# A decoder layer on TensorE: down weights' sums moved into the channel stage, gate weights' parts into the down stage, the first norm into the sixth product, and another order of the pre-products

## The chip, the cores and the metric

The kernel runs on one core of a Trainium2 chip. The metric is the device time of one execution in microseconds (us). PE stands for TensorE (PEld its weight loads), DVE for VectorE, ACT for ScalarE, POOL for GpSimd, SP for SyncE, which here only issues DMAs.

## The reference

One layer of a hybrid decoder (D_MODEL 1024, D_FF 2816) over 1024 prompt tokens and 8 x 4 sample tokens, 1056 together. After the mixing sub-layer (attention and a pooling mixer) come the parts that the change touches:

```python
f = _rms(x, n_ffn_pre)
f = (jax.nn.silu(f @ w_gate) * (f @ w_up)) @ w_down
x = x + _rms(f, n_ffn_post)
x = x + jax.nn.sigmoid(x @ w_ple_gate) * (p @ w_ple)
```

## The kernel before, in words

**Products.** Every fp32 product is made of three passes: each operand is split into a high part, a cast to the matmul type on ACT (`hi`, L185), and a low part, the difference on DVE (`lo`, L186); `gemm` (the matmuls stand at L135) issues hi*hi, hi*lo and lo*hi. Tile names tell the use: wh, wl split weights; sh, sl split sums of weights; qh, ql down weights; w the second weight half of a chunk; xo an activation operand of the down stage; eh one of the gate stage; hl the split of a norm's sum.

**Seven products for eight.** The channel, down and gate stages multiply 2 x 2 blocks by Strassen's scheme in Winograd's form: seven block products P1 to P7, of which four have sums of weight quarters S1 to S4 (`quarter_sums`) and four have sums of activation quarters T1 to T4 as operands. Tokens are cut in two halves of 528 (two matmuls of 264 columns), features in two halves.

**Channel stage.** 22 chunks of 256 channels of D_FF (22 x gate and up). Products P1 and P2 need no sums; they are made ahead, in 44 *pre-products* (`ahead`, L1161): each has a first half (12 matmuls, copied to `st`, L1167) and a second half (`rest`, another 12, copied at L1174 and stored to DRAM, `pd`). Second halves wait in a list; before, a call first issues its own first half and then takes old second halves until 2 (from the eighth call on 1) are left. Split weights live in a pool of 4 pairs, raw ones (wr) in 3 buffers; a split waits for PE to be done with the pair that it overwrites. Then `chunk` (L1204) loads p for chunk c + 2, applies Silu to chunk c's gate part (L1209) and makes the five other products (`seven`). The raw weights' sums are made on POOL (L1124), four operations of 128x512 a chunk, after DVE has made the split `w` from the same buffer; both sums are then split (sh, sl). Results go to DRAM as operands of the down stage (`chunk_put`, L1094). After chunks 3, 7, 11 and 15 `gate_sums` makes on POOL the four sums of a pair of gate weight blocks (tiles ws) and stores them to DRAM (`gd`).

**Down stage.** Seven products of 264 matmuls each, in the order P1, P2, S2, S3, P4, S1, S4 (named by their weights), over 11 slabs taken in groups (`down`, L1301). `x_get` loads the operand of a slab six slabs ahead and splits it. The weight forms of S2, S3, S1 and S4 are made in place on POOL (`down_form`, L316), out of quarters loaded again and one kept for each group. P1 and P2 accumulate in the same four bank pairs, which ACT copies out (L1357, L1359); S2 and all later products take fresh pairs, so they need those copies. The result of the first half of the tokens is complete after P4; its sum of squares is folded and the norm's mean is made by a matmul inside S1 (`rstd_steps`, hl at L421, L422). After S1, `alpha_steps` makes the norm and the gate stage's operands. The second half of the tokens follows after S4 (`beta_steps`).

**Gate stage.** For each of four pairs, P1 and P2 with directly loaded and split weights (W1), then forms S4, S1, S2, S3 and P4 (W2), loaded from `gd` and split in the stage. Sigmoid, product with the embedding, and the store follow.

The order on each engine is set by a scheduler from program order and waits, except for instructions marked `keep_in_program_order`; `turn`, `step` and `chain` spread norm and operand steps over matmuls by rough costs.

Of the kernel before, what the change touches and what calls it, by code (L numbers as in the profile page):

```python
# [17 lines left out]
P = 128  # L18
# [51 lines left out]
def trunk_kernel(  # L70
# [128 lines left out]
    in_a = set()  # L199

    def w_load(j):
        if j >= len(plan) or j in raws:
            return
        src, shape = plan[j]
        t = act_tile(shape) if j in in_a else wpool.tile(shape, F32, tag="wr", bufs=W_RAW, name=nm("wr"))
        queue(nc.sync.dma_start(t, src))
        raws[j] = t
# [57 lines left out]
    QUARTERS = {"P1": ("11", "22"), "P2": ("12", "21"), "S2": ("11",), "S3": ("11", "21"), "P4": ("22",), "S1": ("11",), "S4": ("12",)}  # L265
    OPERAND = {"P1": "B11", "P2": "B21", "P4": "T4", "S2": "T2", "S3": "T3", "S1": "T1", "S4": "B22"}
    WDN, DN_LOADS = {}, {}
    for k in DOWN:
        for e, ps in enumerate(SETS):
            js = []  # L270
            for q in QUARTERS[k]:
                r, c = int(q[1]) - 1, int(q[0]) - 1
                src = w_dn[ps[0] : ps[0] + len(ps), c, :, r, :].rearrange("s p n -> p s n")
                js.append(add_plan(src, [P, len(ps), 512]))
            if k == "P1":
                in_a.add(js[1])
            DN_LOADS[k, e] = tuple(js)
            WDN[k, e] = item("down", k, e)

    PAIRS = ((5, 4), (7, 6), (1, 0), (3, 2))  # L280
    FORMS = ("S2", "S4", "S3", "S1")

    def embed_item(h):
        return direct_item(w_ple[h], [P, 2, 512])

    gate_d = [dpool.tile([P, 4, 2, 512], F32, name=nm("gd")) for _ in range(2)]

    def form_item(k, g):
        if k == "P4":
            b = PAIRS[2 * g][1]  # L290
            src = w_pg[b : b + 3 : 2, :, 4:8, :].rearrange("s p k n -> p s k n")
        else:
            src = gate_d[g][:, FORMS.index(k)].rearrange("p s (k n) -> p s k n", n=P)
        return direct_item(src, [P, 2, 4, P])

    WE, W1 = {}, {}
    for a, _ in PAIRS:
        if a in (5, 1):
            WE[a // 4] = embed_item(a // 4)
        W1[a] = direct_item(w_pg[a], [P, KC, P])  # L300
    LATE = ("S4", "S1", "S2", "S3", "P4")
    W2 = {k: [form_item(k, g) for g in range(2)] for k in LATE}

    made = {}
    until = [len(ITEMS)]
    keeps = {}

    def plans(kind, js):
        return DN_LOADS[js] if kind == "down" else js

    def down_form(k, e):

        r = [raws[j] for j in DN_LOADS[k, e]]

        def add(out, a, b, op):
            ge.tensor_tensor(out, a, b, op=op)  # L316

        if k == "P1":
            keeps[e] = r[1]
        elif k == "P2":  # L320
            add(keeps[e], keeps[e], r[1], ALU.add)
        elif k == "S2":
            add(keeps[e], keeps[e], r[0], ALU.subtract)
            r = [keeps[e]]
        elif k == "S3":
            add(r[0], r[0], r[1], ALU.subtract)
        elif k == "S1":
            add(r[0], keeps[e], r[0], ALU.add)
        elif k == "S4":
            add(r[0], r[0], keeps[e], ALU.subtract)  # L330
        hl = w_tile(r[0].shape, "qh"), w_tile(r[0].shape, "ql")
        split(*hl, r[0])
        return hl

    def need(k, ahead=LOOK):

        for i in range(len(made), max(k + 1, min(k + ahead + 1, until[0]))):
            kind, js = ITEMS[i]
            for j in plans(kind, js):
                w_load(j)  # L340
# [3 lines left out]
            elif kind == "half":  # L344
                t = w_tile([P, KC, P], "w2")
                made[i] = t[:, 0:4, :], t[:, 4:8, :]
                split(*made[i], raws[js[0]][:, 4:8, :])
            elif kind == "down":
                made[i] = down_form(*js)
            else:  # L350
                made[i] = w_sums(*(raws[j] for j in js))
            for kind, js in ITEMS[i + 1 : i + 3]:
                for j in plans(kind, js):
                    w_load(j)
# [635 lines left out]
    def ffn_steps(g):  # L990

        r = yield from rstd_steps(acc[g])
# [168 lines left out]
    def ahead(w, c, i):  # L1161

        wg = need(w)
# [40 lines left out]
    def chunk(c):  # L1204
# [4 lines left out]
        se.activation(c11, c11, AF.Silu)  # L1209
# [62 lines left out]

    def gate_sums(n):

        a, b = PAIRS[n]
        two = []
# [4 lines left out]
        quarter_sums(*two)  # L1281
        for i, t in enumerate(two):
            nc.sync.dma_start(gate_d[n // 2][:, 2 * i : 2 * i + 2, n % 2, :], t.rearrange("p (f k) n -> p f (k n)", f=2))
# [17 lines left out]
    def down(k, banks, onto=False, ends=None, order_=(0, 1, 2, 3), behind=None, far=6):  # L1301

        n0 = DOWN.index(k) * NSLAB
        for es in ((0,), (1,), (2,), (3,), (4, 5)):
# [7 lines left out]
            for j in order_:  # L1312
# [12 lines left out]
                if 5 in es:  # L1325
                    ends(j, banks[j])
                    if behind:
                        behind(j)
# [15 lines left out]
    psum[0] = ctx.enter_context(tc.tile_pool(name="pairs", bufs=4, space=bass.MemoryType.PSUM))  # L1344
    for c in range(FFC):
# [4 lines left out]
        if c % 4 == 3 and c // 4 < len(PAIRS):  # L1350
            gate_sums(c // 4)

    share[0] = 0.5
    queued[:] = [None]
    u = out_half()
    banks = [None] * 4
    down("P1", banks, ends=lambda j, ps: se.copy(at_j(u, j), ps))  # L1357
    os_[0][0] = c11 = out_half()
    down("P2", banks, onto=True, ends=lambda j, ps: se.copy(at_j(c11, j), ps))  # L1359
    sq = half_squares(c11)  # L1360
    down("S2", [None] * 4, ends=lambda j, ps: add(at_j(u, j), at_j(u, j), ps))
    u3 = out_half()
    down("S3", [None] * 4, ends=lambda j, ps: add(at_j(u3, j), at_j(u, j), ps))
    os_[0][1] = c21 = out_half()
    down("P4", [None] * 4, ends=lambda j, ps: add(at_j(c21, j), at_j(u3, j), ps))

    sq2 = half_squares(c21)
    add(sq, sq, sq2)
    folded(0, sq)
    norm = rstd_steps(acc3[0])  # L1370
    next(norm)
    ordered[0] = True
    p5 = out_half()

    def p5_end(j, ps):
        se.copy(at_j(p5, j), ps)

    def norm_behind(j):
        if j == 2:
            next(norm)  # L1380

    down("S1", [None] * 4, ends=p5_end, behind=norm_behind)
    try:
        next(norm)
    except StopIteration as e:
        r = e.value
    ordered[0] = False
    for o in (u3, u):
        for t in range(2):
            add(o[t], o[t], p5[t])  # L1390
    os_[1] = [u, u3]

    def alpha_steps():
        for h in range(2):
            x2_load(0, h)
        for h in range(2):
            operand_tiles(f"B{h + 1}1")
            for t in range(2):
                x2_make(0, h, t, r)
                yield 18, 0  # L1400
                operand_split(f"B{h + 1}1", t, x2[0][h][t])
                yield 8, 0
        ple_operand(0)
        yield 8, 0
        sqb = half_squares(u3)
        folded(1, sqb)
        yield 16, 0

    chain(alpha_steps(), 0)

    def u_end(j, ps):
# [4 lines left out]
        sq = row("sq")  # L1416
        se.activation(sq, v, AF.Square)
        add(by_row(acc3[1]), by_row(acc3[1]), sq)

    down("S4", [None] * 4, ends=u_end, order_=(1, 2, 3, 0), far=4)  # L1420
# [40 lines left out]
    def beta_steps():  # L1461

        norm = rstd_steps(acc3[1])
        next(norm)
        yield
# [54 lines left out]
    for a, _ in PAIRS:  # L1520
        w = need(W1[a], 2)
        ps = product(quarter(w, 0), e7["B11"])
# [12 lines left out]
    for k in LATE:  # L1535
        for g in range(2):
            for i in range(2):
                a, b = PAIRS[2 * g + i]
                w = tuple(t[:, i] for t in need(W2[k][g], 1))
# [124 lines left out]
```

## Time and profile before

| | |
|---|---|
| runs | 1083.18, 1085.08, 1088.99 us |
| median | 1085.08 us |
| profiled execution | 1087.13 us |
| its span, mean granted clock of PE | 1085.3 us, 0.988 |
| PE, DVE, ACT, POOL busy | 97%, 72%, 44%, 25% |
| stages, us from the span's start | attention to 264; pre-products 264 to 407; chunks 409 to 732; down stage to 963; gate stage to the end |
| DMA | 201.75 MB, mean 186 GB/s |

A row of a window gives its length, then busy time and instructions of the engines asked for, the granted clock as a share of full speed, the DMA share and the rate. A row of a timeline gives start, duration, engine, line, operation, output and inputs, and in brackets the idle time ahead of it with what ended it. A row of waits gives total, count and longest. A group's row gives busy time and mean ns, then the idle time before. A DMA row ends with the median us from issue to landing.

### The profile page before, as it was taken

To read this page: it belongs to the slowest core of one execution; us is meant where nothing else is said; L and a number is where in the kernel's file an instruction comes from. 1 tells how busy PE (TensorE), PEld (TensorE's weight loads), DVE (VectorE), ACT (ScalarE), POOL (GpSimd) and SP (SyncE) were. 2 spreads that over 40 slices of the span, in tenths; PEclk is the share of its full clock that TensorE was granted. 3 is DMA by queue.
4 is the path that set the end of the run, shared out by engine and by line. 5 is a ranking of instruction groups with operands and counts; after the bars stand their busy time and mean duration, and the time that the engine had idled before them with its cause. 6 is when DMAs were issued, how large, how long until landed. Compare 5 with 4: busy or idle time off the path is not lost.

```text
span 1085.3 us, 20364 instructions
## 1 busy us (share of the span) xinstructions
PE 1052.8 (97%) x8175; PEld 1032.8 (95%) x8175; DVE 784.2 (72%) x1066; ACT 473.6 (44%) x867; POOL 273.2 (25%) x199
## 2 busy tenths in 40 slices
PE   9999999999799999999999999999989999979997
PEld 8999988899699999999999999999989999979997
DVE  6766378878477944777777776666397568989975
ACT  8522277666476663213232222134363435454621
POOL 1045022200000025464445444401362134200000
PEclk9999999999999999999999999999989999989999
DMA  8121310452588758756474655576685755666443
GB/s 297 59 72 39 115 58 23 156 212 88 176 274 289 243 179 283 251 204 238 168 257 155 239 185 178 167 250 222 193 282 167 259 188 175 229 233 232 130 161 108
DMA packets 110720, 201.75 MB, mean 186 GB/s; under 512 B 8965, under 2 KB 59429, under 8 KB 110625
## 3 DMA queue, kind: packets, MB, share of 16 engines
q1 hardware_dynamic: 109296, 198.68, 54.7%
q10 hardware_dynamic: 1328, 1.77, 0.5%
q8 instruction: 64, 1.05, 0.4%
q14 instruction: 32, 0.25, 0.1%
HBM read 149.08 MB, written 51.34 MB: 185 GB/s over the span
## 4 chain that ended last, share of the span: by engine, by line
PE 73%; DVE 9%; issue 8%; POOL 4%; DMA 3%; ACT 3%; SPq 0%; ACTq 0%; DVEq 0%; POOLq 0%
PE b L135 73%; POOL wr L1124 4%; DVE wl L186 2%; DMA xo<-xd 1%; DVE x L1152 1%; DVE o L1262 1%; DVE eh L186 1%; ACT wh L185 1%; PE b L129 1%; POOL ws L1124 1%; DMA wr<-in_w_gu_dram 1%; DVE u L1152 1%; DMA p<-pd 0%; DMA xr<-in_x_dram 0%; ACT a L767 0%
## 5 line engine op out<-in xcount | busy, mean ns | idle before, releaser
L135 PE MATMUL b<-fh,sh 128*128 128x264 f32 x1408 | 257.8, 284 | 0.1
L135 PE MATMUL b<-xo,qh 128*128 128x264 f32 x1232 | 225.4, 284 | 4.4 <-ACT o L1359 3.4
L135 PEld LDWEIGHTS b<-fh,sh 128*128 128x128 f32 x1408 | 218.4, 189 | 0.8 <-DVE p L1152 0.8
L135 PE MATMUL b<-fh,sl 128*128 128x264 f32 x704 | 199.6, 284 | 0.0
L135 PEld LDWEIGHTS b<-xo,qh 128*128 128x128 f32 x1232 | 191.8, 190 | 5.0 <-ACT o L1359 3.6
L135 PE MATMUL b<-xo,ql 128*128 128x264 f32 x616 | 174.8, 284 | 0.0
L1124 POOL TENSOR_TENSOR wr<-wr 128x512 f32<-128x512 f32 x44 | 56.8, 1291 | 341.0 <-DMA wr<-in_w_gu_dram 187.6
L135 PE MATMUL b<-fh,wh 128*128 128x264 f32 x704 | 130.3, 286 | 4.0 <-ACT wh L185 4.0
L135 PEld LDWEIGHTS b<-fh,sl 128*128 128x128 f32 x704 | 132.9, 189 | 0.0
L186 DVE TENSOR_TENSOR wl<-wr,wh 128x1024 fp32r<-128x1024 f32 (+1 forms) x78 | 96.2, 1235 | 40.0 <-ACT wh L185 39.8
L135 PEld LDWEIGHTS b<-xo,ql 128*128 128x128 f32 x616 | 116.7, 189 | 0.0
L185 ACT CAST wh<-wr 128x1024 fp32r<-128x1024 f32 (+1 forms) x78 | 79.0, 1015 | 85.3 <-PE b L135 79.7
L135 PEld LDWEIGHTS b<-fh,wh 128*128 128x128 f32 x704 | 110.1, 190 | 5.0 <-ACT wh L185 5.0
L135 PE MATMUL b<-h,wh 128*128 128x352 f32 x480 | 113.2, 326 | 1.0 <-ACT h L491 0.7
L185 ACT CAST sh<-wr 128x1024 fp32r<-128x1024 f32 x44 | 45.9, 1043 | 146.1 <-POOL wr L1124 145.2
L186 DVE TENSOR_TENSOR sl<-wr,sh 128x1024 fp32r<-128x1024 f32 x44 | 55.2, 1255 | 73.5 <-ACT sh L185 54.2
L135 PE MATMUL b<-fh,wl 128*128 128x264 f32 x352 | 101.4, 288 | 4.7 <-DVE wl L186 4.6
L186 DVE TENSOR_TENSOR xo<-xo 128x528 fp32r<-128x528 f32 x77 | 69.9, 932 | 49.0 <-ACT xo L185 49.0
L135 PEld LDWEIGHTS b<-h,wh 128*128 128x128 f32 x480 | 83.7, 190 | 2.2 <-DVE h L492 1.3
L185 ACT CAST xo<-xo 128x528 fp32r<-128x528 f32 x77 | 47.6, 632 | 85.3 <-DMA xo<-xd 83.7
L135 PE MATMUL b<-eh,wh 128*128 128x264 f32 x448 | 82.8, 285 | 0.0
L135 PE MATMUL b<-h,wl 128*128 128x352 f32 x240 | 73.9, 325 | 0.0
(184 smaller groups left out, 2066.9 us busy)
## 6 DMA issues: line engine op xcount, KB each, us to landing
wr<-in_w_gu_dram SPq DMA_DIRECT2D x80, 512.0 KB, 4.3
wr<-in_w_dn_dram SPq DMA_DIRECT2D x45, 512.0 KB, 4.0
xo<-xd SPq DMA_DIRECT2D x77, 264.0 KB, 5.0
pd<-st SPq DMA_DIRECT2D x44, 264.0 KB, 4.3
p<-pd SPq DMA_DIRECT2D x22, 528.0 KB, 5.8
xd<-t SPq DMA_DIRECT2D x33, 264.0 KB, 3.7
xd<-c SPq DMA_DIRECT2D x22, 264.0 KB, 2.1
xd<-u SPq DMA_DIRECT2D x22, 264.0 KB, 4.0
```

What stands on the lines that cost most here:

```text
L129: ins = te.transpose(out, src, ident)
L135: ins = te.matmul(*args, **kw)
L185: fix(se.copy(hi, src))
L186: fix(ve.tensor_tensor(lo, src, hi.bitcast(F32), op=ALU.subtract))
L1124: ge.tensor_tensor(out, a, b, op=op)
L1152: ve.tensor_tensor(out, a, b, op=op)
L1262: ve.scalar_tensor_tensor(v, v, gn[:, 3, m : m + 1], by_row(r), op0=ALU.mult, op1=ALU.mult)
```

## The change

It does the following:

1. `ahead` takes old second halves ahead of its new first half, until 4 are left in the first four calls and 1 from then on.
2. The norm ahead of the channel stage, for its second token group, takes its last step later (`refine=35`).
3. The first Silu of the channel stage keeps its place in program order.
4. `down_sums` makes S1, S3, S2 and S4 of the down weights during the chunk stage: per group four quarters are loaded (tiles ds), four POOL operations made (L1285), four results stored to DRAM (`dd`). 20 of 24 are of 128x1024. In the down stage every weight is then one load and one split; `down_form` goes.
5. `gate_sums` moves into the products P1 to S3 of the down stage, in five steps per pair, and now also splits its blocks and sums and stores both parts. In the gate stage W1 and W2 are loaded as split parts (tiles wf) and not split there.
6. In P4, squares of the first half of the tokens are summed as parts of the result come. The norm's steps come inside S1, after the first group of slabs, which is now two groups long (48 matmuls), and `alpha_steps` runs during S1 and S4. S1's result is added from PSUM to both sums rather than copied first. `beta_steps` waits one turn longer before the second norm's mean.

On ACT, at the start of the pre-products, before: st copies of L1167 are first halves, those of L1174 second halves, wh splits of weights.

```order
279 L1167 COPY st_3095<-b_3079 128x264
280 L185 CAST wh_3010<-wr_2928 128x1024
281 L996 ACTIVATE y_2654<-x_2447 128x1408
282 L1174 COPY st_3029<-b_3016 128x264
283 L1167 COPY st_3132<-b_3119 128x264
284 L185 CAST wh_3031<-wr_2982 128x1024
285 L1174 COPY st_3050<-b_3037 128x264
286 L1167 COPY st_3167<-b_3154 128x264
287 L185 CAST wh_3052<-wr_3014 128x1024
288 L1174 COPY st_3071<-b_3058 128x264
```

The same place after; L1143 are first halves and L1147 second halves.

```order
279 L1143 COPY st_3104<-b_3091 128x264
280 L185 CAST wh_3015<-wr_2938 128x1024
281 L1147 COPY st_3036<-b_3021 128x264
282 L969 ACTIVATE y_2664<-x_2457 128x1408
283 L185 CAST wh_3038<-wr_2987 128x1024
284 L1147 COPY st_3062<-b_3044 128x264
285 L1147 COPY st_3083<-b_3070 128x264
286 L185 CAST wh_3064<-wr_3019 128x1024
287 L1143 COPY st_3170<-b_3157 128x264
288 L1147 COPY st_3104<-b_3091 128x264
```

Three second halves now come between the fourth and the fifth first half, where there was one.

On ACT, from the last pre-products to the first chunk, before: `p` is Silu of chunk 0 with the load of its table, `w` and `sh` are splits of chunk 1.

```order
425 L185 CAST w_4504<-wr_4348 128x512
426 L1174 COPY st_4559<-b_4546 128x264
427 L1174 COPY st_4602<-b_4589 128x264
428 L1209 ACT_TABLE_LOAD
429 L1209 ACTIVATE p_4647<-p_4647 128x528
430 L1174 COPY st_4631<-b_4618 128x264
431 L185 CAST sh_4579<-wr_4436 128x1024
```

After:

```order
424 L185 CAST w_4528<-wr_4372 128x512
425 L1147 COPY st_4583<-b_4570 128x264
426 L1143 COPY st_4655<-b_4642 128x264
427 L1147 COPY st_4626<-b_4613 128x264
428 L185 CAST sh_4603<-wr_4460 128x1024
429 L1147 COPY st_4655<-b_4642 128x264
430 L1182 ACT_TABLE_LOAD
431 L1182 ACTIVATE p_4657<-p_4657 128x528
```

Silu has gone behind the last st copy; the split sh of chunk 1 has come ahead of it.

On POOL, at chunk 2's sums (wr_4507 and wr_4587), before:

```order
76 L1124 TENSOR_TENSOR wr_4507<-wr_4507 128x512
77 L1124 TENSOR_TENSOR wr_4507<-wr_4587,wr_4507 128x512
78 L1124 TENSOR_TENSOR wr_4587<-wr_4507,wr_4587 128x512
79 L1124 TENSOR_TENSOR wr_4587<-wr_4587 128x512
80 L1124 TENSOR_TENSOR ws_5363<-ws_5363 128x512
```

After (wr_4531 and wr_4611 are chunk 2's, ds the down weights'):

```order
76 L1097 TENSOR_TENSOR wr_4531<-wr_4531 128x512
77 L1285 TENSOR_TENSOR ds_4860<-ds_4858,ds_4860 128x1024
78 L1097 TENSOR_TENSOR wr_4531<-wr_4611,wr_4531 128x512
79 L1285 TENSOR_TENSOR ds_4858<-ds_4862,ds_4858 128x1024
80 L1097 TENSOR_TENSOR wr_4611<-wr_4531,wr_4611 128x512
81 L1285 TENSOR_TENSOR ds_4862<-ds_4860,ds_4862 128x1024
82 L1097 TENSOR_TENSOR wr_4611<-wr_4611 128x512
83 L1285 TENSOR_TENSOR ds_4864<-ds_4864,ds_4862 128x1024
```

Three down sums now stand between chunk 2's own four; in later chunks one to four stand between two chunks' sums.

The diff, cut to its core:

```diff
-            elif kind == "down":
-                made[i] = down_form(*js)
+            if kind == "loaded":
+                srcs, shape = js
+                made[i] = [w_tile(shape, "wf") for _ in srcs]
+                for t, src in zip(made[i], srcs):
+                    queue(nc.sync.dma_start(t.bitcast(F32), src))
+                continue
...
-        r = yield from rstd_steps(acc[g])
+        r = yield from rstd_steps(acc[g], refine=35 if g == 1 else 10)
...
     def ahead(w, c, i):
+        lag[0] += 1
+        while len(second) > (4 if lag[0] < 5 else 1):
+            second.pop(0)()
         wg = need(w)
         ps = bank()[:, :QN]
         gemm(ps, ops4(quarter(wg, 0), operand("B11", i), i))
         st = row("st")
         se.copy(st[:, 0, :], ps)
-        lag[0] += 1
-        while len(second) > (2 if lag[0] < 8 else 1):
-            second.pop(0)()
...
-        se.activation(c11, c11, AF.Silu)
+        ins = se.activation(c11, c11, AF.Silu)
+        if c == 0:
+            tc.keep_in_program_order(ins)
...
+    def both_parts(dsts, src):
+        shape = [P, *src.shape[1:]]
+        hl = [act_tile(shape, F32R, "ws") for _ in range(2)]
+        split(*hl, src)
+        for dst, t in zip(dsts, hl):
+            nc.sync.dma_start(dst, t.bitcast(F32))
...
+    def down_sums():
+        for e, ps in enumerate(SETS):
+            q = {}
+            for k in ("21", "22", "11", "12"):
+                q[k] = act_tile([P, len(ps), 512], s="ds")
+                nc.sync.dma_start(q[k], down_quarter(k, e))
+            def form(out, a, b, op, k):
+                ge.tensor_tensor(q[out], q[a], q[b], op=op)
+                dst = down_d[e][:, DFORM.index(k)].rearrange("p (s n) -> p s n", n=512)
+                nc.sync.dma_start(dst, q[out])
+            form("22", "21", "22", ALU.add, "S1")
+            yield
+            form("21", "11", "21", ALU.subtract, "S3")
+            yield
+            form("11", "22", "11", ALU.subtract, "S2")
+            yield
+            form("12", "12", "11", ALU.subtract, "S4")
+            yield
...
         chunk(c)
-        if c % 4 == 3 and c // 4 < len(PAIRS):
-            gate_sums(c // 4)
+        for _ in range((24 * (c + 1)) // 20 - (24 * c) // 20):
+            next(sums, None)
...
+    gates = (x for n in range(4) for x in gate_sums(n))
+    def gates_on(e, j):
+        if j == 3:
+            next(gates, None)
...
-    down("P4", [None] * 4, ends=lambda j, ps: add(at_j(c21, j), at_j(u3, j), ps))
+    def c21_end(j, ps):
+        v = at_j(c21, j)
+        add(v, at_j(u3, j), ps)
+        squares_end(c21, 0)(v)
+    down("P4", [None] * 4, ends=c21_end, far=4)
...
-    down("S1", [None] * 4, ends=p5_end, behind=norm_behind)
+    def s1_end(j, ps):
+        for o in (u3, u):
+            add(at_j(o, j), at_j(o, j), ps)
+    down("S1", [None] * 4, ends=s1_end, behind=norm_behind, far=4, groups=((0, 1), (2,), (3,), (4, 5)))
+    os_[1] = [u, u3]
+    folded(1, half_squares(u3))
...
-    down("S4", [None] * 4, ends=u_end, order_=(1, 2, 3, 0), far=4)
+    down("S4", [None] * 4, ends=u_end, far=4)
...
         next(norm)
         yield
+        yield
         next(norm)
```

More of the change, by code (lines that the diff above doesn't have):

```diff
@@ L275, in trunk_kernel @@
[L275 to L278, printed above, removed]
-    PAIRS = ((5, 4), (7, 6), (1, 0), (3, 2))
[L281 to L294, printed above, removed]
@@ L304, in trunk_kernel @@
+    for k in LATE:
+        f = FORMS.index(k)
+        W2[k] = [loaded_item([gate_d[g][:, h, f].rearrange("p s n -> p (s n)") for h in range(2)], [P, 2 * 512]) for g in range(2)]
     made = {}
     until = [len(ITEMS)]
[L306 to L333, printed above, removed]
@@ L1299, in x_get, with down @@
             xops[n] = t
-    def down(k, banks, onto=False, ends=None, order_=(0, 1, 2, 3), behind=None, far=6):
+    def down(k, banks, onto=False, ends=None, order_=(0, 1, 2, 3), behind=None, far=6, groups=((0,), (1,), (2,), (3,), (4, 5))):
         n0 = DOWN.index(k) * NSLAB
-        for es in ((0,), (1,), (2,), (3,), (4, 5)):
+        for es in groups:
             ops = []
@@ L1362, in trunk_kernel @@
+    folded(0, half_squares(c11))
+    down("S2", [None] * 4, ends=lambda j, ps: add(at_j(u, j), at_j(u, j), ps), behind=gates_on)
     u3 = out_half()
-    down("S3", [None] * 4, ends=lambda j, ps: add(at_j(u3, j), at_j(u, j), ps))
+    down("S3", [None] * 4, ends=lambda j, ps: add(at_j(u3, j), at_j(u, j), ps), behind=gates_on)
+    ple_operand(0)
+    for _ in gates:
+        pass
     os_[0][1] = c21 = out_half()
-    down("P4", [None] * 4, ends=lambda j, ps: add(at_j(c21, j), at_j(u3, j), ps))
@@ L1367, in trunk_kernel @@
-    sq2 = half_squares(c21)
-    add(sq, sq, sq2)
-    folded(0, sq)
+    def c21_end(j, ps):
[3 more added lines that the diff above has]
+    down("P4", [None] * 4, ends=c21_end, far=4)
+    for h in range(2):
+        x2_load(0, h)
     norm = rstd_steps(acc3[0])
+    se.activation(tmp(1), epst, AF.Abs_reciprocal_sqrt)
+    ordered[0] = True
     next(norm)
[L1372 to L1376, printed above, removed]
@@ L1378, in norm_behind, with alpha_steps @@
-    def norm_behind(j):
-        if j == 2:
-            next(norm)
-    down("S1", [None] * 4, ends=p5_end, behind=norm_behind)
[L1383 to L1395, printed above, removed]
+    def alpha_steps(r):
         for h in range(2):
@@ L1399, in alpha_steps, with norm_behind @@
                 x2_make(0, h, t, r)
-                yield 18, 0
+                yield 34, 0
                 operand_split(f"B{h + 1}1", t, x2[0][h][t])
[L1402 to L1409, printed above, removed]
+                yield 16, 0
+    def norm_behind(e, j):
+        if e == 0 and j == 1:
+            next(norm)
+        if e == 0 and j == 2:
+            try:
+                next(norm)
+            except StopIteration as x:
+                ordered[0] = False
+                chain(alpha_steps(x.value), 0)
+    def s1_end(j, ps):
[4 more added lines that the diff above has]
+    folded(1, half_squares(u3))
     def u_end(j, ps):
```

85 lines of the change are left out of this document (54 added, 31 removed).

## The prediction

> **What bounds the kernel now.** I read the page's busy times first, then what TensorE (PE) waits for, then its busy time in windows.
>
> ```profile
> PE 1052.8 (97%) x8175; PEld 1032.8 (95%) x8175; DVE 784.2 (72%) x1066; ACT 473.6 (44%) x867; POOL 273.2 (25%) x199
> ...
> PE b L135 <- DVE wl L186: 7.2, 9, 1.0
> PE b L135 <- ACT hl L421: 6.4, 1, 6.4
> PE b L135 <- ACT wh L185: 4.0, 4, 1.1
> PE b L135 <- ACT o L1359: 3.4, 1, 3.4
> PE b L135 <- ACT st L1174: 2.3, 1, 2.3
> ```
>
> PE is the bound: the change leaves the number of matmuls as it is, so it can win only idle time of PE and the slow clock that follows. The windows (us, PE busy and matmuls, granted clock, DMA share, GB/s) price each stall with its aftermath. The first row gives the pace: 323.00/2639 = 0.1224 us a matmul. A window's loss is its length less its matmuls at that pace.
>
> ```profile
> 409.00:732.00 323.00, 322.54 (x2639) 0.99 0.63 214
> 273.00:300.00 27.00, 19.99 (x136) 0.94 0.56 176
> 407.00:415.00 8.00, 5.74 (x35) 0.79 1.03 336
> 797.00:807.00 10.00, 6.62 (x34) 0.66 0.97 342
> 967.00:978.00 11.00, 4.43 (x23) 0.69 0.75 248
> 978.00:1045.00 67.00, 64.47 (x530) 1.00 0.55 182
> ```
>
> Losses: A (273 to 300, first pre-products) 27 - 16.65 = 10.35; C (407 to 415, last pre-product to first chunk) 8 - 4.28 = 3.72; E (797 to 807, second down product to third) 10 - 4.16 = 5.84; F (967 to 978, second norm) 11 - 2.82 = 8.18; G (gate stage) 67 - 64.87 = 2.13. Two single waits join them, B at 328 and D at 737:
>
> ```profile
> 328.09 0.39 PE L135 MATMUL b<-fh,wl 128*128 128x264 f32 x1 [1.03 <-DVE wl L186]
> 737.62 0.36 PE L135 MATMUL b<-xo,qh 128*128 128x264 f32 x1 [0.89 <-DVE u L1152]
> ```
>
> Together 32.1 us are within reach. The chunk stage itself has nothing to win: 322.54 of its 323 us are busy.
>
> **The change part by part.** The sum is made against the profiled execution, 1087.13 us (span 1085.3); the median of the runs, 1085.08, lies 2.05 below.
>
> *A, order of the pre-products: 9.5 won.* In a stall here ACT waits for PE to free a weight pair, splits (wh), DVE makes wl, and PE waits for both:
>
> ```profile
> 284.03 1.04 ACT L185 CAST wh<-wr 128x1024 fp32r<-128x1024 f32 x1 [2.08 <-PE b L135]
> 285.11 1.23 DVE L186 TENSOR_TENSOR wl<-wr,wh 128x1024 fp32r<-128x1024 f32 x1 [5.31 <-ACT wh L185]
> 285.13 0.39 PE L135 MATMUL b<-fh,wh 128*128 128x264 f32 x1 [0.96 <-ACT wh L185]
> ```
>
> Before, the second half that frees the pair came right ahead of the first half that needs it: 2 matmuls (0.24 us) of cover against 1.04 + 1.23 us. Now the second halves of rows 0 to 2 come ahead of first half 4; the next two splits have 26 and 38 matmuls (3.2 and 4.7 us), later ones more. All four stalls and the fifth, small one go; ends 9.0 and 10.35.
>
> *B, first norm's refinement later (refine=35): 1.0 won,* ends 0 and 1.03; DVE's wl no longer queues behind the norm's step that waits for ACT.
>
> *C, Silu of chunk 0 pinned: 2.5 lost.* ACT, then POOL:
>
> ```profile
> 404.20 0.62 ACT L185 CAST w<-wr 128x512 fp32r<-128x512 f32 x1 [1.08 <-PE b L135]
> ...
> 408.36 0.64 ACT L1209 ACTIVATE p<-p 128x528 f32<-128x528 f32 x1 [1.03 <-DMA p<-pd]
> 408.91 0.36 ACT L1174 COPY st<-b 128x264 f32<-128x264 f32 x1
> 411.42 1.05 ACT L185 CAST sh<-wr 128x1024 fp32r<-128x1024 f32 x1 [2.15 <-POOL wr L1124]
> ```
> ```profile
> 406.05 1.28 POOL L1124 TENSOR_TENSOR wr<-wr 128x512 f32<-128x512 f32 x1 [6.80 <-DVE w L186]
> ...
> 410.11 1.28 POOL L1124 TENSOR_TENSOR wr<-wr 128x512 f32<-128x512 f32 x1
> ```
>
> The last st copy frees a bank that the first chunk product needs. Before, it stood behind Silu, which waited for its load; PE idled 2.26 us. Now Silu is behind it, but so far as the order of ACT shows, the split sh of chunk 1 is ahead of it, and that waits for POOL's four sums (406.05 to 411.39, 5.34 us), which begin 1.85 us after the cast w. The cast can start 36 matmuls (4.4 us) ahead of PE's last one. So the sums end 5.34 + 1.85 - 4.4 = 2.8 us after it, sh takes 1.05, st 0.36: PE resumes after about 4.1 us, 1.9 later than before. To that I add 0.6 for the clock; ends +3.7 (the stall goes) and -3.9 (a second slow window).
>
> ```profile
> 410.70:414.10 3.40, 3.40 (x18) 0.50 1.06 383
> ```
>
> After a gap of 2.26 us the granted clock was 0.50 for 3.4 us, with 18 matmuls where the pace gives 28. The Trainium skill, "TensorE: Matmul & The Clock Gate", Part 1, has the clock halve only after an idle window of about 3.4 us; this row shows it after less. By the page the slow window would be new with a gap of 4.1 us, so C would lose about 1.2 us more than by the row; I go by the row.
>
> *Chunk stage, down weights' sums: 1.5 lost.* 20 POOL operations of 128x1024 and 4 of half that come in, the 16 of the gate weights go. Groups of POOL operations, the window of the stage, and DVE and PE rows of chunks 2 and 4, where POOL works on both kinds of sums:
>
> ```profile
> L316 POOL TENSOR_TENSOR wr<-wr,wr 128x1024 f32<-128x1024 f32 x5 | 12.8, 2566 | 25.2 <-DMA wr<-in_w_dn_dram 25.2
> L1124 POOL TENSOR_TENSOR ws<-ws,ws 128x512 f32<-128x512 f32 x8 | 13.6, 1701 | 0.6
> ...
> 409.00:732.00 323.00, 322.54 (x2639) 321.92 (x2640) 229.87 (x282) 85.45 (x115) 139.12 (x98) 0.99 0.63 214
> 409.00:424.00 15.00, 14.68 (x108) 14.68 (x109) 5.54 (x7) 6.12 (x10) 4.51 (x4) 0.89 0.97 344
> ...
> 428.61 2.07 DVE L186 TENSOR_TENSOR sl<-wr,sh 128x1024 fp32r<-128x1024 f32 x1 [1.59 <-ACT sh L185]
> 476.86 1.79 DVE L1094 TENSOR_TENSOR u<-u,u 128x528 f32<-128x528 f32 x1
> 480.28 0.69 DVE L1152 TENSOR_TENSOR p<-p,b 128x528 f32<-128x528 f32 x1
> ...
> 442.98 0.28 PE L135 MATMUL b<-fh,sh 128*128 128x264 f32 x1
> ```
>
> In: 20 x 2.57 and 4 at half of that, 57 us; out: 16 x 1.70 = 27. POOL goes from 139 us of 323 (last but one column of the window row: PE, PEld, DVE, ACT, POOL) to about 170. A DVE operation with two SBUF operands took 1.79 us beside it, 0.69 with one operand from PSUM. The gate sums came four at a time (some 7 us) and PE lost nothing that the first window shows; three or four of the new ones in a row are 7.7 to 10 us. Three stand ahead of the last of chunk 2's own sums. Their cover: chunk 2's first split was ready at 428.61 + 2.07 = 430.68, PE used it at 442.98, 12.3 us later. That holds against 7.7, not against 5 us more, from a DVE that runs late or from the first down quarters, which are loaded about 409 to 424, with DMA at 0.97. Ends 0 and 6 (a quarter us for each of the 24); nearest is the gate sums' cost, so I take a low value.
>
> *E and D, down stage: 4.0 and 0.5 won.* POOL's 30 form operations and the second loads go; POOL gets 16 smaller ones, ACT and DVE 20 splits in P1 to S3, SP their loads and stores. ACT's copies o at 800 were late because its xo splits waited for loads; SP now passes gate stores that wait for splits. Ends 0 and 5.84, 0 and 0.9. Bytes: 18.9 MB of gate loads and stores come, 8.7 MB of second down loads go, 77 GB/s over 133 us:
>
> ```profile
> 732.00:867.00 135.00, 130.73 (x1061) 130.34 (x1060) 86.52 (x86) 54.52 (x80) 43.07 (x18) 0.97 0.68 224
> ...
> xo<-xd SPq DMA_DIRECT2D x77, 264.0 KB, 5.0
> ```
>
> About 300 GB/s, below the 344 seen from 409 to 424. The xo loads are asked for six slabs ahead (144 matmuls, 17.6 us, at least) and took 5.0. I charge 1.0; ends 0 and 5.
>
> *F, norms: 7.8 won, 0.5 lost.* What the second norm waited for (ACT, DVE):
>
> ```profile
> 973.12 0.63 ACT L421 CAST hl<-acc 128x528 fp32r<-128x528 f32 x1 [3.18 <-DVE acc L1152]
> ...
> 971.25 1.22 DVE L186 TENSOR_TENSOR wl<-wr,wh 128x1024 fp32r<-128x1024 f32 x1
> 972.39 0.70 DVE L1152 TENSOR_TENSOR acc<-acc,sq 128x528 f32<-128x528 f32 x1
> 973.78 0.71 DVE L422 TENSOR_TENSOR hl<-acc,hl 128x528 fp32r<-128x528 f32 x1 [0.70 <-ACT hl L421]
> ```
>
> DVE was behind with the operands of the first half of the tokens (norm and splits), now made during S1 and S4. The mean's matmul now has 60 matmuls (7.3 us) ahead of it after S4, where the remaining chain is add 0.70, square 0.64 (as the Silu of that size above), add 0.70, hl 0.63 and 0.71, 3.4 us, and up to two wl of 1.22: 5.8. Ends 6.5 and 8.18. The first norm's mean now stands 48 matmuls (5.9 us) into S1 against such a chain with a table load: 0 to 2 lost, 0.5 taken.
>
> *G, gate parts loaded ready: 2.1 won, 1.0 lost.*
>
> ```profile
> L186 DVE TENSOR_TENSOR wl<-wr,wh 128x1024 fp32r<-128x1024 f32 x12 | 14.7, 1222 | 1.6 <-ACT wh L185 1.6
> wr<-gd SPq DMA_DIRECT2D x8, 512.0 KB, 4.0
> ```
>
> These splits leave the stage, and the waits for them (ends 1.0 and 2.13). But each item now loads two 512 KB parts into buffers that PE frees; four items have about 50 matmuls (6.1 us) from that to their use, against 4.0 for a load, some 0.5 to ask for it and about 1 more for the second: 0 to 1 us each.
>
> Sum: 9.5 + 1.0 - 2.5 + 4.0 + 0.5 + 7.8 + 2.1 = 22.4, less 1.5 + 1.0 + 0.5 + 1.0 = 4.0: 18.4 us. 1087.13 - 18.4 = 1068.7, and 2.05 less as a median: **1067 us**.
>
> **The rivals.** *R1, slower: POOL holds DVE in the chunk stage.* If a new sum delays the DVE operation for which PE waits, PE pays for it. Without the chunk term 19.9 us are won; from (19.9 + 5.4)/24 = 1.05 us an operation the kernel is slower by over 0.5%; at 1.6 each, 38 us, it takes about 1103. For: 1.79 instead of 0.69 above, with longer operations now. Against: the gate sums' groups, and DVE idle 29% of the stage. Chance 0.07. The Trainium skill, "SBUF — State Buffer", Who interferes with whom, states it as an exclusive lock on a shared port pair, held for the whole instruction; 1.79 agrees.
>
> *R2, about the same: late operands in the down stage.* If gate traffic holds up xo loads, E stays and comes again at the next two hand-overs: 4.0 + 2 x 5.84 = 15.7 less, about 1082. For: E itself fell in a window with DMA at 0.97. Against: the mean rate. Chance 0.13.
>
> *R3, faster: the stall C goes,* if chunk 1's sums are ready earlier than I work out: 2.5 + 3.7 more, about 1061. Chance 0.10.
>
> **How the numbers follow.** Forecast 0.70, R1 0.07, R2 0.13, R3 0.10. A measurement here tells about 0.5% (5.4 us) from no change. Faster: forecast's 0.67, R3's 0.10, a quarter of R2, 0.80. Same: the rest of R2 and a little of the forecast's bad ends, 0.12. Slower: R1 and 0.01, 0.08. The range runs from R3 with E in full and nothing lost to chunks and loads (1060.5 - 1.8 - 1.5 - 1.0 = 1056) to R2 with 2 us more for the chunks (1084).
>
> **What would show it.** Right: no waits for wh and wl between 273 and 300, none for hl near the second norm, none for wl in the gate stage; a gap of about 4 us before the first chunk product, for st, with ACT's sh behind POOL ahead of it; chunk stage within 2 us of 2639 x 0.1224. Wrong: PE waiting for DVE p or u many times among the chunks (R1); waits for ACT o or xo at several hand-overs (R2); waits for wf loads of over 1 us.

## The result and the profile after

The changed kernel takes 1098.53 us (median of 4 runs, 1096.57 to 1099.91) against 1085.12 for the kernel before (the three runs above and a fourth, 1085.17): 1.0118 times as long (95% interval 1.0084 to 1.0152). It is slower, and the forecast of 1067 us was wrong. The profiled execution took 1097.2 us. Busy time of PE, then what it waits for:

```profile
PE 1051.0 (96%) x8175; PEld 1030.7 (94%) x8175; DVE 764.5 (70%) x1074; ACT 475.6 (43%) x870; POOL 255.9 (23%) x193
```
```profile
PE b L135 <- DVE p L1125: 21.8, 10, 7.9
PE b L135 <- ACT st L1147: 5.2, 1, 5.2
PE b L135 <- DVE o L1125: 2.9, 1, 2.9
PE b L135 <- ACT p L1552: 1.8, 2, 1.0
PE b L135 <- DMA wf<-ge: 1.7, 2, 1.0
...
PE b L135 <- DMA wf<-gd: 0.7, 1, 0.7
PE b L135 <- DVE xo L186: 0.6, 2, 0.4
```

The waits for the norm's hl (L421), wh, wl and ACT's o are gone. In their place stands one that the kernel before did not have: for DVE's p, the addition that empties a PSUM bank which the next product of a chunk needs. Windows (us, PE busy and matmuls, clock, DMA share, GB/s) of the first pre-products, the end of the pre-products, the first 323 us of the chunks, their last 24 us with the down stage's first 120, and the end of its fourth product:

```profile
273.00:300.00 27.00, 27.00 (x226) 1.00 0.96 314
391.00:403.00 12.00, 6.80 (x44) 0.86 0.70 225
403.00:726.00 323.00, 301.24 (x2418) 0.97 0.67 230
726.00:870.00 144.00, 143.70 (x1196) 1.00 0.84 293
870.00:890.00 20.00, 16.58 (x121) 0.91 0.91 316
```

The first is full now. The third, as long as the window of the chunks before, holds 2418 matmuls instead of 2639. From the first matmul of each stage to that of the next one (in the gate stage, to the end of the last matmul), the stages last:

| us | pre-products | chunks | down | gate |
|---|---|---|---|---|
| before | 144.8 | 322.9 | 230.7 | 116.9 |
| after | 134.8 | 351.5 | 229.0 | 110.6 |

So 18.0 us are won in three stages and 28.6 lost in the chunk stage, net 10.6 (the profiled executions differ by 10.1). The place of the loss is that of rival R1; whether its mechanism is R1's was the question for the chip.

**One stall, followed back.** The longest wait for p, rows of PE, DVE, ACT, POOL and SP:

```profile
515.31 0.59 PE L135 MATMUL b<-fh,sh 128*128 128x264 f32 x1 [7.90 <-DVE p L1125]
...
510.81 1.23 DVE L186 TENSOR_TENSOR sl<-wr,sh 128x1024 fp32r<-128x1024 f32 x1 [13.06 <-ACT sh L185]
...
514.55 0.70 DVE L1125 TENSOR_TENSOR p<-p,b 128x528 f32<-128x528 f32 x1
...
509.74 1.04 ACT L185 CAST sh<-wr 128x1024 fp32r<-128x1024 f32 x1 [18.95 <-POOL wr L1097]
...
493.56 5.21 POOL L1285 TENSOR_TENSOR ds<-ds,ds 128x1024 f32<-128x1024 f32 x2 [6.06 <-DMA ds<-in_w_dn_dram]
498.74 1.28 POOL L1097 TENSOR_TENSOR wr<-wr 128x512 f32<-128x512 f32 x1
503.39 2.39 POOL L1285 TENSOR_TENSOR ds<-ds,ds 128x1024 f32<-128x1024 f32 x1 [3.38 <-issue]
505.74 2.63 POOL L1097 TENSOR_TENSOR wr<-wr,wr 128x512 f32<-128x512 f32 x2
508.44 1.26 POOL L1097 TENSOR_TENSOR wr<-wr 128x512 f32<-128x512 f32 x1
...
487.53 0.34 SPq L1287 DMA_DIRECT2D dd<-ds  x1
...
488.40 0.72 SPq L1282 DMA_DIRECT2D ds<-in_w_dn_dram  x1
...
498.80 0.38 SPq L1282 DMA_DIRECT2D ds<-in_w_dn_dram  x1
```

Read from below: SP asks for a quarter of the down weights at 488.40, only behind the store of an earlier sum; POOL waits for it 6.06 us. A chunk's own four sums (wr) stand behind these two down sums, and the last three of them behind a third one. That one starts 3.38 us late; the view names no cause, but the load asked for at 498.80 lands at 503.27 in this trace. ACT's sh waits for the last of the four, DVE's sl for sh, and p, for which PE has stood 7.9 us when it goes on, comes behind sl and four other sums on DVE. In another stall (462.38) there is no waiting in line, but POOL beside DVE, where a sum of two SBUF operands takes 2.91 us instead of 0.70:

```profile
462.38 0.39 PE L135 MATMUL b<-fh,sh 128*128 128x264 f32 x1 [2.45 <-DVE p L1125]
...
452.59 11.35 POOL L1285 TENSOR_TENSOR ds<-ds,ds 128x1024 f32<-128x1024 f32 x4
...
456.01 2.91 DVE L1125 TENSOR_TENSOR u<-u,u 128x528 f32<-128x528 f32 x1
```

And in a third (579.12) ACT stands at a chunk's Silu, whose p load comes late, with other ACT work behind it:

```profile
574.55 0.65 ACT L1182 ACTIVATE p<-p 128x528 f32<-128x528 f32 x1 [2.99 <-DMA p<-pd]
```

Of the 21.8 us, by what stood ahead of p, 12.6 are of the first kind (four waits), 4.8 of the second (three), 4.4 of the third (three). The other 6.8 us of the 28.6 are matmuls at a slower clock: over the whole stage PE is busy for 329.7 us at a mean granted clock of 0.97, before for 322.8 at 0.99, with the same number of matmuls. These kinds are readings; the runs below test them. Their names there: order (POOL's queue), port (POOL holding DVE), ACT (the Silu with its late load). The times below are medians of four or more runs beside the kernel before on the same chip, with the ratio to that; the length of a stage comes from one profiled execution. The median of the kernel before lies between 1084.67 and 1089.22 us from one set of runs to the next, so a difference of a few us between two runs of different sets is near the noise.

### The profile page after: what moved, and what is told of

Same layout as the page of the kernel before. It is cut to its first block, busy times and chain, and to the rows that moved or that the text cites. A ratio compares the mean times of both kernels' runs of the same rounds, so it can differ in the third digit from the quotient of the medians.

```text
span 1095.2 us, 20452 instructions
## 1 busy us (share of the span) xinstructions
PE 1051.0 (96%) x8175; PEld 1030.7 (94%) x8175; DVE 764.5 (70%) x1074; ACT 475.6 (43%) x870; POOL 255.9 (23%) x193
## 4 chain that ended last, share of the span: by engine, by line
PE 58%; DMA 12%; issue 10%; DVE 8%; POOL 6%; ACT 4%; SPq 1%; ACTq 0%; POOLq 0%; DVEq 0%
PE b L135 58%; POOL wr L1097 4%; DMA xo<-xd 3%; DMA ds<-in_w_dn_dram 2%; POOL ds L1285 2%; DMA wr<-in_w_gu_dram 2%; DVE u L1125 1%; DVE sl L186 1%; DMA dd<-ds 1%; DVE fr L1015 1%; ACT sh L185 1%; DVE c L1125 1%; DVE t L1067 1%; DMA wr<-in_w_ple_dram 1%; DMA xr<-in_x_dram 1%
## 5 line engine op out<-in xcount | busy, mean ns | idle before, releaser
L135 PE MATMUL b<-fh,sh 128*128 128x264 f32 x1408 | 263.6, 288 | 21.8 <-DVE p L1125 21.8
L135 PE MATMUL b<-xo,wh 128*128 128x264 f32 x1232 | 224.4, 283 | 3.7 <-DVE o L1125 2.9
L135 PEld LDWEIGHTS b<-xo,wh 128*128 128x128 f32 x1232 | 190.6, 188 | 4.8 <-ACT xo L185 3.5
L135 PE MATMUL b<-xo,wl 128*128 128x264 f32 x616 | 174.0, 282 | 0.0
L186 DVE TENSOR_TENSOR wl<-wr,wh 128x1024 fp32r<-128x1024 f32 (+1 forms) x106 | 127.2, 1204 | 41.3 <-ACT wh L185 40.0
L185 ACT CAST wh<-wr 128x1024 fp32r<-128x1024 f32 (+1 forms) x106 | 105.4, 997 | 97.3 <-PE b L135 77.8
L135 PEld LDWEIGHTS b<-xo,wl 128*128 128x128 f32 x616 | 116.0, 188 | 0.0
L186 DVE TENSOR_TENSOR xo<-xo 128x528 fp32r<-128x528 f32 x77 | 56.6, 749 | 46.9 <-ACT xo L185 44.1
L135 PE MATMUL b<-eh,wf 128*128 128x264 f32 x672 | 85.0, 283 | 4.2 <-ACT p L1552 1.8
L135 PEld LDWEIGHTS b<-eh,wf 128*128 128x128 f32 x672 | 82.3, 187 | 5.5 <-ACT p L1552 2.2
```

What stands on the lines that cost most here:

```text
L135: ins = te.matmul(*args, **kw)
L185: fix(se.copy(hi, src))
L186: fix(ve.tensor_tensor(lo, src, hi.bitcast(F32), op=ALU.subtract))
```

## The experiments

**What the sums cost as a whole, and what their traffic costs.** Leaving out the sums with all their DMAs (e1), and the POOL operations alone (e2):

```diff
-    sums = down_sums()
+    sums = iter(())                       # e1; weights' source: plain quarters
...
-                ge.tensor_tensor(q[out], q[a], q[b], op=op)      # e2
```

> The changed kernel without the down weights' sums in the chunk stage: no loads, no POOL operations and no stores of them; the down stage loads plain quarters of the same size in their place (so its products are not the forms'). It prices what these sums cost as a whole. If the cost is in them, however it arises, PE's waits for DVE p (21.8 us, ten of them) and the slow clock behind them go, and the time falls by the 33 us that the chunk stage lost, to about 1066. If the loss comes from elsewhere (the pre-products' order, the later start of the chunks), the waits for p stay and the time is above 1090.

> The changed kernel with the loads and stores of the down weights' quarters kept in the chunk stage, but without the 24 POOL operations between them (plain quarters are stored). Queue theory (POOL's own sums for the chunks stand behind down sums that wait for loads; ACT's sh, DVE's sl and then DVE's p stand behind those) and port theory (POOL's long operations hold DVE's) both expect the waits for p to be nearly gone, at most 4 us of late p loads, and 1066 to 1072. The traffic theory (22 MB more through DMA delays what PE needs) expects most of the 21.8 us to stay, above 1088.

e1 takes 1063.93 us (0.9793, 0.9739 to 0.9846), e2 1065.75 (0.9807, 0.9756 to 0.9857); the chunk stage lasts 322.7 and 322.9 us, as before, and neither has a wait for p. After the change, e1 and e2, in the same stretch of the stage:

```profile
403.00:723.00 320.00, 298.24 (x2393) 0.97 0.67 232
403.00:723.00 320.00, 320.00 (x2631) 1.00 0.55 183
403.00:723.00 320.00, 320.00 (x2628) 1.00 0.74 255
```

So the sums cost the kernel 33 to 35 us, and the 23 MB that e2 moves more than e1 (233.99 against 210.92) cost nothing by themselves: the traffic theory is out. The loss needs POOL's 24 operations.

**POOL's operations without their loads (e3).**

```diff
-            q = {}
+            if e == 0:          # four tiles, loaded once; no stores
+                q = {}
```

> The changed kernel with the 24 POOL operations kept, on four tiles that are loaded once, without the other loads and without stores (the down stage loads plain quarters). POOL works as long as before on the down sums but never waits for a load of theirs. Port theory: DVE's operations stay as long beside them, waits for p of 15 us or more in all, about 1085 to 1095. Queue theory: the waits behind a load (7.9 us at once, and some later) go, and those from three or four operations in a row stay: 3 to 8 us of waits, 1070 to 1080.

It takes 1104.37 us (1.0161, 1.011 to 1.0213), outside both expectations. With its operands always there, the scheduler had moved the sums together: POOL's rows, and PE's longest wait.

```profile
438.48 20.99 POOL L1287 TENSOR_TENSOR ds<-ds,ds 128x1024 f32<-128x1024 f32 x8
459.43 1.26 POOL L1097 TENSOR_TENSOR wr<-wr 128x512 f32<-128x512 f32 x1
...
469.97 1.26 POOL L1097 TENSOR_TENSOR wr<-wr 128x512 f32<-128x512 f32 x1
```
```profile
483.12 0.59 PE L135 MATMUL b<-fh,sh 128*128 128x264 f32 x1 [28.19 <-DVE p L1125]
```

Fifteen down sums stand ahead of the end of one chunk's own four, eleven of them in the rows shown. That shows what the order on POOL can cost, but the order was not held fixed, so it does not tell the kinds apart.

**The split ahead of the last st copy (e4).** A dependency without a wait puts the first split behind the copy, and the last pre-products ask for one split less ahead:

```diff
+        if last_st:
+            tc.add_manual_dep(ins.ins, last_st.pop(), NOSYNC, reason="order of copies")
...
-            ahead(w, c, i)
+            ahead(w, c, i, LOOK - (w == WA[-1]))
```

> The changed kernel with one order edit on ACT: the split sh of chunk 1's sums comes behind the last st copy of the pre-products, no longer ahead of it. If the 5.2 us wait for st ahead of the first chunk product comes from that place in ACT's queue alone, it falls to under 0.5 us, its slow clock goes, and the time falls by 5 to 7 us, to 1092 to 1094. If the bank is late for another reason, the wait stays above 2 us and the time falls by less than 3.

1085.84 us (0.9984, 0.9959 to 1.0009). The wait for st falls from 5.2 to 0.5 us, as expected. The time falls by 12.7, more than the 5 to 7 for it: the pre-products take 131.5 us instead of 134.8, but the chunks 342.9 instead of 351.5. The edit had also moved some down sums on POOL (waits for p 16.5 us instead of 21.8), and the stage's slow clock behind the wait for st goes as well (its first 24 matmuls took 4.57 us), so how the rest of the gain divides between this copy and POOL's order was not separated. e4 is the base of what follows.

**An even order on POOL (f1), and variants of it.**

```diff
-                ge.tensor_tensor(q[out], q[a], q[b], op=op)
+                tc.keep_in_program_order(ge.tensor_tensor(q[out], q[a], q[b], op=op))      # f1
```

> The changed kernel with the split of chunk 1's sums behind the last st copy (as in e4_sum_later), and with the 24 down sums kept in program order on POOL: one of them, seldom two, behind each four chunk sums instead of up to four in a row and between a chunk's own four. POOL's work, loads and stores are the same. Order theory: what costs PE is that a chunk's sums stand behind down sums (ACT's sh, DVE's sl and DVE's p then wait in line): waits for p fall from 16.5 us to under 4, and the time from 1086 to 1062 to 1068. Port theory: the same 24 operations hold DVE as before, waits for p of 10 us or more stay, 1078 to 1086.

> As f1_pinned, but each down sum is two memsets of its tile (POOL writes and reads nothing; the down stage gets constants), in the same places in POOL's order, with the same loads and stores. Port theory: without two-operand reads on POOL beside them DVE's operations keep their length, so this is faster than f1_pinned by 5 us or more, 1062 to 1068. Order theory: within 3 us of f1_pinned.

> As f1_pinned, with each down sum of 128x1024 made as two of 128x512 right behind one another, same sums. Port theory: each hold is half as long and DVE gets in between, so this is 3 us or more faster than f1_pinned. Order theory: within 2 us of f1_pinned, about 1062 to 1068.

f1 takes 1103.49 us (1.0175, 1.0129 to 1.0221), f3 1118.64 (1.0319, 1.0274 to 1.0363), f2 1075.62 (0.9913, 0.9883 to 0.9942). My order theory fell here: with one down sum, three times two, between one chunk's sums and the next one's, the kernel is 18 us slower than e4. In the chunk stage PE now waits 19.8 us for DVE's u and 10.5 for p. What f1 waits for on SP in the chunk stage, and ACT ahead of Silu:

```profile
SPq L1293 <- POOL ds L1291: 200.7, 24, 14.4
```
```profile
  DMA p<-pd: 115.5, 17
```

Against, in the changed kernel:

```profile
SPq L1287 <- POOL ds L1285: 29.5, 7, 7.5
...
SPq L1157 <- DMA dd<-ds: 16.4, 5, 5.8
```
```profile
  DMA p<-pd: 49.5, 12
```

and 18.7 us for Silu in the kernel before. All 24 stores stand on SP until POOL has made their sum, p loads behind them; ACT stands 115 us at Silu. Halved sums are no help: 1.67 us each beside DVE is more than half of the 2.45 of a whole one. f2, with two memsets in place of a sum, is 27.9 us faster than f1, far more than the 5 us that the port theory asked for: its chunk stage lasts 335.3 us instead of 360.2, and DVE's sl takes 1.23 us in the mean instead of 1.73. But POOL's work is also shorter there (42 us instead of 55), and SP's wait for it at the stores falls from 200.7 to 99.4 us, so f2 does not tell the port from the queues.

**The stores, and all their DMAs, on POOL's queue (g1, g2, k5).**

```diff
-                nc.sync.dma_start(dst, q[out])
+                nc.gpsimd.dma_start(dst, q[out])      # g1 on e4, g2 on f1; k5 on e4, the loads too
```

> As e4_sum_later, with one edit: the stores of the down sums are issued by POOL, behind the sum itself, and no longer by SP. SP theory (new, after f1_pinned was slower: a store on SP waits for its POOL sum, and the loads behind it on SP, p for ACT's Silu and weights, come late; ACT's queue stands at Silu, with the casts sh and w behind it): SP no longer waits for ds, waits for DVE p fall from 16.5 us to under 8, and the time from 1086 to 1072 to 1078. Port theory: POOL's sums hold DVE as before, 1083 to 1090.

> As f1_pinned (one down sum behind each four chunk sums, 1103 us), with the stores issued by POOL. SP theory: the 200 us that SP waited for ds there are gone, and with the even order nothing is left but a little port contention: 1062 to 1070. Port theory: 24 sums hold DVE as in f1_pinned, 1090 or more.

> As e4_sum_later, with the loads of the down weights' quarters and the stores of their sums both issued by POOL: SP's queue holds none of them. ACT theory: SP waits for no down sum except where a p tile takes over a slot, ACT's idle time for p loads falls from 55 us to under 30, and the time to 1068 to 1080. POOL theory: POOL has the same sums and 48 issues of 0.58 us more, 1090 or above.

1103.34 (1.0167, 1.0146 to 1.0187), 1111.61 (1.0246, 1.0221 to 1.0272) and 1107.29 us (1.02, 1.0181 to 1.0219): all slower than their bases, and a miss for the theory as I had put it. In g1 SP no longer waits for the sums at the stores but at p loads and quarter loads, whose tile slots a down sum or its store still holds; in k5 its p loads wait 61.1 us for such stores. In k5 POOL issues everything, 0.6 to 0.7 us of POOL each, and waits itself:

```profile
L1291 POOL TENSOR_TENSOR ds<-ds,ds 128x1024 f32<-128x1024 f32 x20 | 49.0, 2450 | 44.5 <-DMA ds<-in_w_dn_dram 44.4
L1288 POOL DMA_DIRECT2D ds<-in_w_dn_dram x24 | 17.2, 717 | 19.3 <-DMA dd<-ds 12.8 <-issue 4.4 <-POOL ds L1291 2.0
```

So moving the wait from SP to POOL, whose queue also holds the chunk sums, is worse, and the p loads stay late because of shared slots.

**ACT's order (k3, k4).** The p loads may be late if nothing needed stands behind Silu on ACT. Every Silu of p is kept in program order, behind the casts of the next chunk:

```diff
         ins = se.activation(c11, c11, AF.Silu)
-        if c == 0:
-            tc.keep_in_program_order(ins)
+        tc.keep_in_program_order(ins)      # k3 on e4, k4 on f1
```

> As e4_sum_later (1086 us, waits for DVE p 16.5 us), with every chunk's Silu of p kept in program order on ACT: behind the casts w and sh of the next chunks, not ahead of them. POOL's and SP's order stay as they are. ACT theory (p loads come late because SP stands at DMAs of the down sums; ACT stands at Silu, and the casts sh and w that DVE and PE need stand behind it): waits for p fall to under 6 us and the time to 1070 to 1076. POOL theory (POOL's sums hold DVE at the port, or chunk sums come late in POOL's order): 1083 to 1089.

> As f1_pinned (down sums kept in program order on POOL, 1103 us), with every Silu kept in program order on ACT as well. ACT theory: the late p loads no longer hold the casts, 1065 to 1080. POOL theory: 1095 or more.

k4 takes 1075.77 us (0.9906, 0.9882 to 0.9929), 27.7 less than f1, with the same orders on POOL and DVE and only somewhat shorter waits on SP:

```profile
SPq L1292 <- POOL ds L1290: 170.3, 24, 9.8
```
```profile
PE b L135 <- DVE p L1129: 6.4, 4, 3.0
```

Its chunk stage lasts 329.2 us, f1's 360.2. Of the p loads none ends an idle time of ACT any more. That shows ACT's queue as a path by which, in f1's order on POOL, late loads reach PE. f2 had won nearly as much with that queue as it was, so the gains of the two cannot be added. k3 takes 1079.26 (0.9943, 0.9921 to 0.9966), 6.6 less than e4, but its chunk stage lasts 340.4, only 2.5 less: with the scheduler's POOL order, which is e4's to the last operation, p still waits 11.6 us, a miss for the ACT theory on its own. Each mend alone leaves the other queue in the way (POOL's order +17.3 us in the stage, ACT's -2.5); both together win 13.7.

**What is left: the port (m1).** As k4, with memsets, which read nothing, in place of the sums:

```diff
-                tc.keep_in_program_order(ge.tensor_tensor(q[out], q[a], q[b], op=op))
+                for _ in range(3):
+                    tc.keep_in_program_order(ge.memset(q[out], 0.5))
```

> As k4_both_pinned (1076 us), with each down sum replaced by three memsets of its tile (about 2.9 us, longer than the 2.5 of the sum; POOL writes and reads nothing; the down stage gets constants). Orders, loads and stores stay. Port theory for the rest: DVE's sl and u are back at 1.23 and 0.70 us, the chunk stage loses under 5 us, 1064 to 1068. If the rest comes from SP's queue and late loads, POOL being as long, it stays at 1074 or more.

1071.46 us (0.9844, 0.9798 to 0.9891; k4's own median 1075.77). DVE's splits beside it, first k4, then m1, and POOL's memsets:

```profile
L189 DVE TENSOR_TENSOR sl<-wr,sh 128x1024 fp32r<-128x1024 f32 x40 | 67.6, 1691 | 56.9 <-ACT sh L185 54.6 <-PE b L135 2.2
```
```profile
L189 DVE TENSOR_TENSOR sl<-wr,sh 128x1024 fp32r<-128x1024 f32 x40 | 49.0, 1224 | 61.7 <-ACT sh L185 31.8 <-PE b L135 29.9
...
L1291 POOL MEMSET ds<- 128x1024 f32 x60 | 57.2, 956 | 2.3
```

With POOL busy longer, DVE's splits are as short as without any sums (1.23 us in e1). The stage shortens by 3.0 us, to 326.2, the whole kernel by 4.3. So the port is real: with POOL's and ACT's orders mended, the sums' reads cost PE some 3 us. That is a small difference between single executions of different sets, and the reads are not all that differs. SP's wait for POOL at the stores is half as long as in k4, where it was 170.3 us:

```profile
SPq L1293 <- POOL ds L1291: 84.3, 22, 4.6
```

Part of the 3 us may come that way. The result lies between the two expectations: 3.4 us over e1's stage remain, or rather more, since e1's stage also holds the slow clock behind its wait for st (17 matmuls from 400 to 404 us, 36 in m1). PE waits 6.3 us for DVE's u at the last two chunks and the start of the down stage. What causes these waits was not tried.

**The parts that won, on the kernel before.** The order of the pre-products alone (a1); with e4's edit (b1); with the second norm's mean a turn later too (b2); and parts 1, 2 and 6 with e4's edit (h1).

```diff
+        lag[0] += 1
+        while len(second) > (4 if lag[0] < 5 else 1):      # a1, ahead of need(w)
+            second.pop(0)()
...
-        lag[0] += 1                                        # a1, behind the st copy
-        while len(second) > (2 if lag[0] < 8 else 1):
-            second.pop(0)()
...
         next(norm)
         yield
+        yield                                              # b2
```

> The kernel before with the new order of the pre-products alone. The stalls from 273 to 297 us go (9 to 10 us won). On ACT this order by itself brings the split sh of chunk 1 ahead of the last st copy, without the pinned Silu: if that is what made the wait for st longer (5.2 us instead of 2.3, with a longer slow clock), it does so here too, 4 to 5 us lost, 1079 to 1081. If the pinned Silu is the cause, the wait stays near 2.3 us and the time is 1075 to 1076.

> As a1_order (the kernel before with the new order of the pre-products, 1074 us), with the split sh of chunk 1 put behind the last st copy. The 5.2 us wait for st falls to 0.5 and its slow clock goes: 1067 to 1070. If the wait's cost is taken up by a later stall, 1072 or more.

> As b1_order_copy (1068 us), with the second norm's mean one turn later in the gate stage, as in the changed kernel: 24 matmuls (2.9 us) more ahead of it. The wait of 6.7 us for hl falls to about 4 and the slow clock shortens: 1063 to 1066. If DVE only shifts and the splits behind it wait instead, no change: 1067 to 1069.

> The kernel before with the pre-products' order, the later refinement, the norms' change (parts 1, 2 and 6) and the split of chunk 1's sums behind the last st copy; the down sums stay in the down stage and the gate sums in the chunk stage. If these parts win what the trace of the changed kernel shows (10 us of stalls among the pre-products, 1 behind them, 8 at the second norm) and the late st copy goes (3.5), it takes 1061 to 1065. If the norms' change needs the freed POOL or the gate stage without splits, a stall for hl of 3 us or more stays and it takes 1068 or more.

a1 takes 1074.00 us (0.9895, 0.9859 to 0.9931), b1 1068.16 (0.9843, 0.9821 to 0.9864), b2 1069.24 (0.9829, 0.978 to 0.9877), h1 1071.66 (0.9876, 0.9853 to 0.9899). In a1 the wait for st is there without a pinned Silu:

```profile
PE b L135 <- ACT hl L421: 6.8, 1, 6.8
PE b L135 <- ACT st L1174: 5.2, 1, 5.2
```

so the new order makes it, not Silu; in b1 it is 0.5. a1 won more than expected: beside the stage of pre-products (135.2 us instead of 144.8) the chunk stage is 1.9 us shorter and the down stage 1.5, where the stall at the second product's end was 1.3 instead of 3.4 us. b2 cannot be told from b1: the wait for hl goes, and waits for ACT's p and a split in the gate stage come (5.0 and 2.3 us in all). h1 with the early norm is not faster than b1: its down stage takes 236.5 us instead of 226.5, with a wait of 5.8 us for DVE's o ahead of S4. b1 and b2 beat both kernels of this study.

## Why the prediction was wrong

- **The step that failed: "Chunk stage, down weights' sums: 1.5 lost", ends 0 and 6.** It lost 28.6 us, and e1 and e2 show that this goes with POOL's 24 operations. I compared POOL's time (7.7 us) with the slack of the chunk sums (12.3 us) as if the quarters were in place and SP free; in the longest stall POOL first waited 6.06 us for a quarter that SP had asked for late. The gate sums were the wrong nearest row: 16 small operations, for which SP waited 4.4 us in all:

```profile
SPq L1283 <- POOL ws L1124: 4.4, 2, 3.6
```

  The new sums close a ring of in-order queues: a store on SP waits for POOL, loads for POOL and ACT stand behind it, chunk sums stand behind down sums on POOL, casts behind Silu on ACT, p behind sl on DVE. From the changed kernel's chunk stage (351.5) to k4's (329.2) 22.3 us go: 8.6 with e4's edit, which moved POOL's order too, and 13.7 with POOL's and ACT's orders mended together. The 6.3 us that are left over the kernel before are not explained in full.
- **R1** had the sign, the place and nearly the time (1103), and PE waits for p among the chunks as it said. How much of the 28.6 us is its mechanism, the port, stays open. By the reading above it is 4.8 of 21.8 us of waits in the changed kernel; memsets in place of the sums win 3.0 us of the stage in k4's order, but 24.9 in f1's, with POOL's work shorter as well; and no run made that exchange in the changed kernel's own order. That the time came near was partly luck: R1 assumed 1.6 us an operation, and 28.6 us are 1.19 for each of the 24.
- **A and B** were right: the stage of pre-products shortens by 10.0 us although C grew, and no stall of their kinds is left. B's step is not what did it, though: in a1, which has the new order but not refine=35, the wait at 328 is gone as well, so B's 1.0 us came out right by luck and the later refinement was not shown to win anything. One wait of 0.93 us for a first half's st copy at 384 is new; a1 has it too (0.94).
- **C** was right in sign and size: resuming was expected after 4.1 us of idling, it took 5.2; with it mended, the stage of pre-products is 3.3 us shorter (e4). I put it down to the pinned Silu; a1 shows that the order of the pre-products does it.
- **D and E** were right: both waits are gone (in a1, too, E's wait was only 1.3 us, by a change far ahead of it). A new wait of 2.93 us for DVE's o came at 881, between the fourth and the fifth product, where gate and operand splits stand ahead of it on DVE. The stage wins 1.7 us, 3 were expected.
- **DMA** in P1 to S3 (749.74 to 877) ran at 299 GB/s (300 expected) with no wait for xo above 0.4 us: R2 did not happen.
- **F and G**: the wait for hl is gone, the loaded parts cost 2.4 us of waits (1.0 expected), and ACT's p 1.8. The gate stage, with the second norm in it, wins 6.3 us; 8.9 were expected.

## What to carry to other kernels

A new operation on an idle engine is not priced by that engine's free time: list what stands behind each of its waits in every in-order queue, the stores and the slots that it frees among them. When orders come from a scheduler, look at what an edit does to orders elsewhere, and mend two coupled queues together, since either mend alone can look useless or harmful. To test contention, replace the operation by one that keeps the queue and lacks the suspected access, look at what else moved with it, and do it in the kernel's own order: here the same exchange was worth 3 us in one order and 25 in another.

## What the runs showed of the hardware

A memset on POOL beside DVE leaves a two-operand DVE operation at 1.224 us, where among POOL's sums it takes 1.69 in the mean, with the same operations kept in order (m1 and k4). The Trainium skill, "SBUF — State Buffer", Who interferes with whom, says that such DVE operations contend only with POOL instructions that read SBUF; these two runs agree.

A DVE sum of two SBUF operands (128x528) takes 0.70 us by itself. Where it begins while a POOL sum runs, it ends 0.56 to 0.59 us after that sum ends, however much of it was left: so it was in all 34 such places of the kernel before, all 27 of the changed one and all 17 of k4. Two of them in the changed kernel: u begins at 456.01 and ends at 458.92, POOL's ds at 458.35; t begins at 603.61 and ends at 606.51, POOL's ds at 605.95. With one operand from PSUM none of the 225 such operations that begin beside a POOL sum in these kernels took more than 0.71 us. This is the hold that R1 argued with; what it cost the changed kernel is the open part. The hold works the other way as well: the ds that ends at 458.35 took 3.27 us instead of 2.4; it began at 455.08, while DVE's sl (453.74 to 456.09) was still running.
